# A hybrid decoder layer on one core: four latencies of the planner that orders the attention phase

## The chip, the cores and the metric

The kernel runs on one core of a Trainium2 chip. Times are device microseconds (us) of that core, one launch of the whole layer, and the median of several runs counts. Engines are named as in the profile: PE is TensorE (PEld its weight loads), DVE is VectorE, ACT is ScalarE, POOL is GpSimd, and SP issues most of the DMAs. A bulk product below is one 128x128 by 128x272 matmul of the projections (line L301); a small product is any other matmul.

## The reference, cut to what matters

One decoder layer for a prompt of 512 tokens and for 8 samples of 4 tokens each, in float32, width 1024. Feed-forward, token mixer, feed-forward, each between norms. The change lies in the mixer.

```python
def token_mixer(h, pos, conv_buf, S0, attend, p):
    proj = h @ p['w_in']
    u, z, b_raw, a_raw, q_sw, k_sw, v_sw, gate_a, gate_b = jnp.split(proj, split_idx, axis=-1)
    u, conv_new = short_conv(u, conv_buf, p['conv_w'])        # conv_new is an output, too
    ...
    o_dn, S_new = gated_delta_rule(q_dn, k_dn, v_dn, g, beta, S0)
    o_dn = (rmsnorm(o_dn, p['dn_norm']) * silu(z)).reshape(B, T, DN_V)
    ...
    o_sw, kbuf_new, vbuf_new = attend(q, k, v, p['sinks'])    # prompt: band of 128; sample: cache + own rows
    y = sigmoid(gate_a) * o_dn + sigmoid(gate_b) * o_sw
    return y @ p['w_out'], (kbuf_new, vbuf_new, conv_new, S_new)

def swa_banded(q, k, v, sinks):                               # per group g and 128-query block
    scores = jnp.einsum('bnqkgd,bnskd->bnkgqs', qb, kk) * (SW_HEAD_DIM ** -0.5)
    p = sink_softmax(scores, mask, sinks.reshape(SW_KV_HEADS, SW_GROUP))
    o = jnp.einsum('bnkgqs,bnskd->bnqkgd', p, vv).reshape(B, T, SW_Q)
```

## The kernel before, in words

A float32 product is made of three products of rounded halves: weights arrive by DMA as `raw`, ACT rounds them to `hi` (L270), DVE or POOL takes `lo = raw - hi` (L271), and `mm3` (L301) issues hh*hi, hl*hi and hh*lo, each once for each half of the 544 columns (512 of the prompt, 32 of the samples). So a trace shows pairs of bulk products, and each pair has one weight block.

In the mixer the projections with `w_in` are the main stream. They run in a fixed order of units: four blocks U0 to U3 of the convolved q, k, v of the delta branch, two heads each; between them K, V and the two halves of Q; then eight units G0 to G7 of gates; then `w_out`. Beside the main stream run side streams, all Python generators: two of prompt attention (`attend_stream`, the second one goes on with `attend_sample`), two of the delta rule (`delta_stream`, two heads at a time), one `conv_out` for each head, the delta rule of the samples (`delta_sample`) and the merges.

A planner, class `Streams`, puts all of them in one order. It has a clock `now` in its own units. The main stream yields costs; a side stream yields (cost, latency) between its steps, and its next step falls due when the clock has passed `now + LATK * latency`, with LATK = 1.5. After each step of the main stream every side step that is due is emitted. That order of emission is the priority of the instructions; a scheduler, which has a model of the engines, then fixes the order on each engine. Engines run their queue strictly in that order, and an instruction whose operand isn't there holds up all behind it.

The steps that matter here:

- `conv_block` finishes a head's convolution: ACT copies the projection out (L1183), POOL copies the ends (L1186 to L1189, tile `c`), ACT and DVE make the taps (`y`, L1192, L1194), ACT the tanh (`th`, L1197), DVE the product (`kq` or `vT`, L1198). `conv_out` follows L_CVO later: PE turns `c` (`pco`, L1212), DVE copies it (`so`, L1214), two DMAs write it.
- `attend` does one block of 128 queries for one group of heads: scores `psc` (L1012), mask and maximum on DVE (L1016), the steps L1022 to L1035 on DVE with the exponentials on ACT (L1030), the scaling `s` (L1039 on ACT for one quarter, L1042 on DVE for the rest), the turn of the probabilities on PE (`ppt`, L1051), copies (L1057, L1059), the output `pov` (L1065). There are 16 blocks, eight in each of the two streams, and `ppt` comes 5.5 * L_ATT after the scaling was emitted.
- `attend_sample` does the samples in three items of 3, 3 and 2: scores `pss` (L1098, L1100), softmax, turns `psp`, `psn` (L1126, L1127), then the output products `pso` (L1141, L1146), four groups one straight after the other, then the copies to `osw` (L1150).
- `delta` ends with `pro` (sums of squares), the reciprocal root `ro0y` or `ro1y` on DVE (eleven small instructions, L340 to L345), and 3.5 * L_DN later `prb`, the broadcast of the root by PE (L353), which scales `od` (L1370). Ahead of that, `inverse` inverts 128x128 triangles by substitution on DVE (L1420, L1422), with turned copies `XL` (L1433), and by many small products on PE (`pw` L1440 and L1464, `pz` L1448 and L1478, `pt` L1451 and L1474).

`rope` (L936 to L941) turns the projected queries and keys on DVE. L_ATT is 1.0 and L_DN 0.9.

## Time and profile before

| what | value |
|---|---|
| runs | 1606.12, 1608.23, 1611.68 us; median 1608.23 |
| profiled execution | 1608.77 us, its span 1607.0 us |
| busy, of the span | PE 96%, DVE 55%, ACT 40%, POOL 19% |
| mixer, 720 to 760 us | PE 33.76 of 40 us, DVE 34.61 |
| mixer, 840 to 880 us | PE 38.48 of 40 us, DVE 38.23 |
| granted PE clock, mean of the span | 0.983 |

The profiled execution lies 0.54 us above the median, and 1.77 us of it are outside the span. [...] The views below give, for a stretch, the busy time of each engine and the clock; for an engine, its instructions in order, with the idle time before each and what ended it; and the waits summed up.

### The profile page before, as it was taken

What the parts mean: (1) busy time and instruction counts of PE and PEld (TensorE: products, weight loads), DVE (VectorE), ACT (ScalarE), POOL (GpSimd) and SP (SyncE); (2) the same over time, 40 slices, a digit from 0 to 9 for tenths busy, and PEclk for the clock granted to TensorE, in tenths of its full rate; (3) what the DMA queues carried; (4) which work ended last, traced back from release to release, by engine and by line L of the source; (5) the groups of instructions that cost most, each with busy time, mean ns of one, the idle gap of its engine ahead of it and who ended that gap; (6) DMA issues with size and microseconds to landing.
All of it is one profiled execution on the core that took longest, in us unless ns stands there. A gap on an engine that the chain in (4) does not pass through costs nothing.

```text
span 1607.0 us, 33057 instructions
## 1 busy us (share of the span) xinstructions
PE 1537.5 (96%) x12851; PEld 1418.5 (88%) x12851; DVE 887.6 (55%) x2384; ACT 640.1 (40%) x1449; POOL 305.9 (19%) x443
## 2 busy tenths in 40 slices
PE   7999999999998999998999999999979999999996
PEld 4799999999977999997778888889979999999995
DVE  5433322333598787688889568665474332233365
ACT  4322222222445544445575242223556332223363
POOL 2000000000343231231122134131458000000042
PEclk9999999999999999999999899999999999999998
DMA  9554445445655334653113243624515432333353
GB/s 314 169 183 138 153 136 159 147 148 153 190 167 178 100 75 107 165 135 77 45 45 80 77 121 83 167 55 130 158 53 158 115 86 87 94 87 89 83 152 111
DMA packets 316083, 199.69 MB, mean 124 GB/s; under 512 B 37508, under 2 KB 298335, under 8 KB 315638
## 3 DMA queue, kind: packets, MB, share of 16 engines
q1 hardware_dynamic: 315638, 197.46, 43.5%
q8 instruction: 101, 1.65, 0.4%
q14 instruction: 56, 0.46, 0.1%
q0 software_dynamic: 288, 0.11, 0.0%
HBM read 182.08 MB, written 16.36 MB: 123 GB/s over the span
## 4 chain that ended last, share of the span: by engine, by line
PE 77%; DVE 13%; ACT 3%; DMA 2%; issue 2%; POOL 2%; SPq 0%; DVEq 0%; ACTq 0%; POOLq 0%
PE pg L301 16%; PE pu L301 16%; PE pb L301 16%; PE pd L301 14%; PE adaps L467 3%; DVE y L1194 2%; DVE lo L271 2%; ACT hi L270 1%; PE pov L1065 1%; DVE X L1422 1%; PE pgu L301 1%; DVE s L1016 1%; PE psc L1012 1%; PE pkq L1281 1%; DVE xT L571 1%
## 5 line engine op out<-in xcount | busy, mean ns | idle before, releaser
L270 ACT CAST hi<-raw 128x512 fp32r<-128x512 f32 (+2 forms) x502 | 287.9, 581 | 613.1 <-PE pu L301 172.1
L271 DVE TENSOR_TENSOR lo<-raw,hi 128x512 fp32r<-128x512 f32 (+2 forms) x368 | 252.9, 688 | 385.8 <-ACT hi L270 378.7
L301 PE MATMUL pb<-hh,hi 128*128 128x272 f32 (+1 forms) x1008 | 234.9, 303 | 1.4 <-ACT hi L270 0.7
L271 POOL TENSOR_TENSOR lo<-raw,hi 128x512 fp32r<-128x512 f32 (+1 forms) x104 | 140.6, 1356 | 483.1 <-ACT hi L270 460.5
L301 PE MATMUL pb<-hh,lo 128*128 128x272 f32 (+1 forms) x1008 | 227.7, 296 | 1.3 <-POOL lo L271 0.7
L301 PE MATMUL pb<-hl,hi 128*128 128x272 f32 (+1 forms) x1008 | 227.2, 295 | 1.0 <-DVE hl L271 1.0
L301 PEld LDWEIGHTS pb<-hh,hi 128*128 128x128 f32 (+1 forms) x1008 | 164.6, 191 | 12.0 <-issue 6.5
L301 PE MATMUL pd<-fh,hi 128*128 128x272 f32 x704 | 171.3, 290 | 0.0
L301 PE MATMUL pd<-fl,hi 128*128 128x272 f32 x704 | 170.2, 289 | 0.0
L301 PEld LDWEIGHTS pb<-hl,hi 128*128 128x128 f32 (+1 forms) x1008 | 165.0, 190 | 3.6 <-DVE hl L271 1.5
L301 PEld LDWEIGHTS pb<-hh,lo 128*128 128x128 f32 (+1 forms) x1008 | 164.4, 191 | 4.1 <-DVE lo L271 1.4
L301 PE MATMUL pd<-fh,lo 128*128 128x272 f32 x672 | 162.4, 289 | 4.0 <-POOL lo L271 2.2
L301 PE MATMUL pg<-hh,hi 128*128 128x272 f32 x672 | 149.6, 292 | 7.5 <-ACT hh L538 3.6
L301 PE MATMUL pu<-hh,hi 128*128 128x272 f32 x672 | 148.2, 291 | 0.0
L301 PE MATMUL pg<-hl,hi 128*128 128x272 f32 x672 | 147.0, 289 | 0.3 <-DVE hl L539 0.2
L301 PE MATMUL pu<-hl,hi 128*128 128x272 f32 x672 | 146.1, 289 | 0.0
L301 PE MATMUL pu<-hh,lo 128*128 128x272 f32 x672 | 145.3, 288 | 0.7 <-POOL lo L271 0.7
L301 PE MATMUL pg<-hh,lo 128*128 128x272 f32 x672 | 145.6, 288 | 0.0
L301 PEld LDWEIGHTS pd<-fh,hi 128*128 128x128 f32 x704 | 119.9, 188 | 8.6 <-issue 4.2
L301 PEld LDWEIGHTS pg<-hh,hi 128*128 128x128 f32 x672 | 108.8, 189 | 19.6 <-ACT hh L550 5.0
L301 PEld LDWEIGHTS pd<-fl,hi 128*128 128x128 f32 x704 | 120.2, 188 | 0.0
L301 PEld LDWEIGHTS pd<-fh,lo 128*128 128x128 f32 x672 | 114.1, 188 | 5.6 <-POOL lo L271 2.9
(469 smaller groups left out, 2628.6 us busy)
## 6 DMA issues: line engine op xcount, KB each, us to landing
raw<-w_in SPq DMA_DIRECT2D x136, 256.0 KB, 3.2
wa<-w_ada SPq DMA_DIRECT2D x56, 512.0 KB, 4.4
raw<-ffn_w_gate SPq DMA_DIRECT2D x94, 256.0 KB, 2.9
raw<-ffn_w_up SPq DMA_DIRECT2D x94, 256.0 KB, 7.0
raw<-ffn_w_down SPq DMA_DIRECT2D x92, 256.0 KB, 3.0
wb<-w_ada SPq DMA_DIRECT2D x32, 256.0 KB, 5.8
S<-state_delta SPq DMA_DIRECT2D x8, 512.0 KB, 8.0
delta_sample<-S SPq DMA_DIRECT2D x8, 512.0 KB, 3.4
```

The source lines that it names most:

```text
L270: self.nc.scalar.copy(out=hi, in_=raw)
L271: (eng or self.nc.vector).tensor_tensor(out=lo, in0=raw, in1=hi.bitcast(F32), op=ALU.subtract)
L301: self.nc.tensor.matmul(out=ps[:m, c, :TH], lhsT=a[:r, kt, :m], rhs=b[:r, kx, c * TH:(c + 1) * TH], start=first and i == 0, stop=last and ...
L467: self.ada_mm = nc.tensor.matmul(out=ps[32 * j:32 * j + 32, :], lhsT=self.cT[:, k, :], rhs=was[j], start=k == 0, stop=k == 7, skip_group_c ...
L571: nc.vector.tensor_tensor(out=self.xT[:, b, s], in0=self.xT[:, b, s], in1=t[:, :n], op=ALU.add)
L1012: nc.tensor.matmul(out=ps[:, i * 256:i * 256 + nk], lhsT=self.qT[64 * h:64 * h + 64, 2 * g + i, qb * P:(qb + 1) * P], rhs=self.kd[64 * h:6 ...
L1016: nc.vector.tensor_tensor_reduce(out=s[:, i, :nk], in0=ps[:, i * 256:i * 256 + nk], in1=am[:, lo:], scale=0.125, scalar=-3e38, op0=ALU.add ...
L1065: nc.tensor.matmul(out=po[64 * h:64 * h + 64, :256], lhsT=self.vn[:, c, 64 * g:64 * g + 64], rhs=pTs[kb][:, 2 * h:2 * h + 2, :], start=kb ...
L1194: nc.vector.scalar_tensor_tensor(out=y[:, :CVN], in0=cv[:, i:i + CVN], scalar=w[i], in1=y[:, :CVN], op0=ALU.mult, op1=ALU.add)
L1281: nc.tensor.matmul(out=pv[:, j], lhsT=kq[:, n, 0, c * P:(c + 1) * P], rhs=kq[:, n, :, c * P:(c + 1) * P], start=True, stop=True)
L1422: e.tensor_tensor(out=xs, in0=xs, in1=pv, op=ALU.subtract)
```

## The change

Four constants or yields of the side streams change; no arithmetic does, and the instructions are the same.

- `conv_out` falls due 4.0 instead of 2.0 latencies after it was spawned (3 units of the planner later).
- The first block of each of the two attention streams adds L_FIRST = 6.0 to the latency ahead of its `ppt` (9 units).
- `attend_sample` yields after each of its four groups of output products, with latency L_PSO = 0.6, where it yielded once, after the copies.
- The latency from `pro` to `prb` is 5.0 * L_DN instead of 3.5 * L_DN (2 units).

```diff
-L_CVO = 2.0
+L_CVO = 4.0
+L_FIRST = 6.0
+L_PSO = 0.6
...
-    def attend(self, g, qb, tp):
+    def attend(self, g, qb, tp, first):
...
-        yield 0.0, 5.5 * L_ATT
+        yield 0.0, 5.5 * L_ATT + first * L_FIRST
...
-        for g, qb in items:
-            yield from self.attend(g, qb, tp)
+        for n, (g, qb) in enumerate(items):
+            yield from self.attend(g, qb, tp, n == 0)
...
+                yield 0.2 * n, L_PSO
             for h in range(2):
...
-            yield 0.6 * (n + 1), 0.0
...
-        yield 0.85, 3.5 * L_DN
+        yield 0.85, 5.0 * L_DN
```

Lines of the changed kernel are two higher from the constants on (L301 is L303). Below are pieces of the order that the two programs have on an engine.

First place: PE at the turn of the first two attention blocks, 48 bulk products into G0. Names: `pco` turns a head's conv rows `c`, `ppt` turns the probabilities `s`, `pov` and `psc` are outputs and scores, `pw` belongs to an inverse. Before:

```order
L301 MATMUL pb<-hh,lo 128x272 x2
L1051 MATMUL ppt<-ident,s 128x128 x8
L301 MATMUL pb<-hh,hi 128x272
L1051 MATMUL ppt<-ident,s 128x128 x4
L1065 MATMUL pov<-pT,vn 64x256 x4
L1012 MATMUL psc<-kd,osw 128x256 x4
L1065 MATMUL pov<-pT,vn 64x256 x2
L1012 MATMUL psc<-kd,osw 128x256 x4
L1212 MATMUL pco<-ident,c_8741 81x128
L301 MATMUL pb<-hh,hi 128x272
```

After:

```order
L1214 MATMUL pco<-ident,c_8712 81x128
L303 MATMUL pb<-hl,hi 128x272 x2
L303 MATMUL pb<-hh,lo 128x272 x2
L1053 MATMUL ppt<-ident,s 128x128 x8
L303 MATMUL pb<-hh,hi 128x272
L1053 MATMUL ppt<-ident,s 128x128 x4
L1067 MATMUL pov<-pT,vn 64x256 x4
L1014 MATMUL psc<-kd,osw 128x256 x4
L1067 MATMUL pov<-pT,vn 64x256 x2
L1014 MATMUL psc<-kd,osw 128x256 x4
L1442 MATMUL pw_9144<-XL,O 32x32 x16
L303 MATMUL pb<-hh,hi 128x272
```

The `ppt` have the same bulk product ahead of them as before. Two `pco` of other heads now stand ahead of them, and the one that followed them is gone from there; the first small products of an inverse (`pw`) came up from 50 bulk products further on.

Second place: DVE where the root `ro1y` of the first heads is finished (the three passes are L343 to L345; two lines higher in the changed kernel), beside the rope steps and the delta products `NT`, `AT`. Before:

```order
L936 TENSOR_TENSOR y_8187<-x_8183,cs 128x272
L271 TENSOR_TENSOR lo<-raw,hi 128x512
L937 TENSOR_TENSOR w<-x_8184,cs 128x272
L343 SCALAR_TENSOR_TENSOR ro1a<-rx,ro1y 128x4
L1285 SCALAR_TENSOR_TENSOR NT<-pkq,b_8290,Dm 128x128
L938 TENSOR_TENSOR y_8187<-y_8187,w 128x272
L939 TENSOR_TENSOR x_8184<-x_8184,cs 128x272
L940 TENSOR_TENSOR w<-x_8183,cs 128x272
L344 TENSOR_TENSOR ro1a<-ro1a,ro1y 128x4
L1287 TENSOR_TENSOR AT<-pkq,Dm 128x256
L941 TENSOR_TENSOR x_8184<-x_8184,w 128x272
L345 SCALAR_TENSOR_TENSOR ro1y<-ro1a,ro1y 128x4
```

After:

```order
L347 SCALAR_TENSOR_TENSOR ro1y<-ro1a,ro1y 128x4
L345 SCALAR_TENSOR_TENSOR ro1a<-rx,ro1y 128x4
L346 TENSOR_TENSOR ro1a<-ro1a,ro1y 128x4
L347 SCALAR_TENSOR_TENSOR ro1y<-ro1a,ro1y 128x4
L938 TENSOR_TENSOR y_8187<-x_8183,cs 128x272
L273 TENSOR_TENSOR lo<-raw,hi 128x512
L939 TENSOR_TENSOR w<-x_8184,cs 128x272
L1287 SCALAR_TENSOR_TENSOR NT<-pkq,b_8312,Dm 128x128
L940 TENSOR_TENSOR y_8187<-y_8187,w 128x272
```

The last pass of `ro1y` was behind the rope steps and is now ahead of them. On PE the `prb` that reads it stands 7 bulk products earlier than before.

Third place: PE at the output products of the first sample item (`pso`), in G2. Before:

```order
L301 MATMUL pb<-hh,lo 128x272 x2
L1141 MATMUL pso<-spN,vn 64x48 x2
L1146 MATMUL pso<-spT,vc 64x16 x6
L1141 MATMUL pso<-spN,vn 64x48 x2
L1146 MATMUL pso<-spT,vc 64x16 x6
L1141 MATMUL pso<-spN,vn 64x48 x2
L1146 MATMUL pso<-spT,vc 64x16 x6
L1141 MATMUL pso<-spN,vn 64x48 x2
L1146 MATMUL pso<-spT,vc 64x16 x6
L1474 MATMUL pt_11334<-W,X 32x32 x4
L1478 MATMUL pz_11333<-X,W 32x32 x4
```

After, from the first group to the second:

```order
L1143 MATMUL pso<-spN,vn 64x48 x2
L1148 MATMUL pso<-spT,vc 64x16 x6
L1214 MATMUL pco<-ident,c_10855 81x128
L303 MATMUL pb<-hh,hi 128x272 x2
L303 MATMUL pb<-hl,hi 128x272 x2
L303 MATMUL pb<-hh,lo 128x272 x2
L303 MATMUL pb<-hh,hi 128x272 x2
L303 MATMUL pb<-hl,hi 128x272 x2
L303 MATMUL pb<-hh,lo 128x272 x2
L1480 MATMUL pz_11304<-X,W 32x32 x4
L1488 MATMUL pw_11355<-XL,NT 64x64 x4
L1143 MATMUL pso<-spN,vn 64x48 x2
```

Before, no bulk product stood between the four groups. Now 12 stand between one group and the next, and the same holds for the second and third item. Of the small steps between the groups, `pz` and `pw` belong to an inverse.

Elsewhere the order differs as follows, in bulk products: the first four `pco` stand 24 later; the attention and delta steps that follow the first place stand 10 to 50 earlier; the sample's delta chain stands 36 to 190 later, and its last step, the `prb` of the second half of the heads, 72 later, which leaves 24 bulk products of G7 behind it.

## Rows read from the trace of the kernel before

**Rows 1.** The page: busy time by engine.

```profile
PE 1537.5 (96%) x12851; PEld 1418.5 (88%) x12851; DVE 887.6 (55%) x2384; ACT 640.1 (40%) x1449; POOL 305.9 (19%) x443
```

**Rows 2.** Stretches: length, busy PE, PEld, DVE, ACT, POOL (instructions), PE clock, DMA share, GB/s.

```profile
589.00:617.00 28.00, 23.62 (x176) 22.19 (x176) 26.33 (x80) 11.99 (x21) 7.56 (x21) 1.00 0.33 75
692.00:737.00 45.00, 43.14 (x315) 41.60 (x315) 42.43 (x120) 18.34 (x35) 14.31 (x37) 0.96 0.47 108
744.00:890.00 146.00, 142.01 (x1403) 115.44 (x1402) 128.25 (x540) 90.00 (x285) 25.82 (x58) 0.98 0.24 61
911.00:1076.00 165.00, 159.12 (x1672) 143.33 (x1673) 110.86 (x367) 50.27 (x143) 50.48 (x61) 0.96 0.40 104
```

**Rows 3.** Waits of PE, 560 to 760 us, by releaser: total, times, longest.

```profile
PE ppt L1051 <- issue: 6.1, 1, 6.1
PE pco L1212 <- POOL c L1189: 2.5, 2, 1.8
PE prb L353 <- DVE ro1y L345: 1.9, 1, 1.9
...
PE pb L301 <- ACT cv L1183: 0.5, 1, 0.5
```

**Rows 4.** Timeline of DVE at 617 us: start, length, instruction, idle before, releaser.

```profile
616.88 2.62 DVE L1194 SCALAR_TENSOR_TENSOR y<-cv,cwT,y 128x600 f32<-128x600 f32 x2 [0.94 <-ACT y L1192]
```

**Rows 5.** Timeline of DVE, 697 to 704 us: two passes of the root.

```profile
697.68 0.15 DVE L345 SCALAR_TENSOR_TENSOR ro1y<-ro1a,ro1y 128x4 f32<-128x4 f32 x1
...
702.44 1.22 DVE L345 SCALAR_TENSOR_TENSOR ro1y<-ro1a,ro1y 128x4 f32<-128x4 f32 x1
```

**Rows 6.** Stretches of 4 or 5 us, as in group 2.

```profile
704.00:708.00 4.00, 4.00 (x23) 4.00 (x22) 3.90 (x9) 2.15 (x9) 0.10 (x1) 0.57 0.73 200
745.00:750.00 5.00, 5.00 (x26) 2.83 (x26) 4.78 (x15) 2.65 (x6) 1.26 (x1) 0.64 0.49 131
885.00:890.00 5.00, 5.00 (x84) 4.29 (x83) 3.13 (x6) 1.58 (x3) 0.00 (x0) 0.86 0.22 52
890.00:895.00 5.00, 5.00 (x47) 4.62 (x47) 2.68 (x14) 0.37 (x1) 0.00 (x0) 0.50 0.52 150
895.00:900.00 5.00, 4.98 (x58) 4.37 (x56) 2.21 (x5) 1.85 (x4) 0.21 (x1) 0.96 0.12 33
920.00:925.00 5.00, 5.00 (x44) 4.49 (x42) 0.93 (x8) 1.11 (x3) 0.31 (x1) 0.50 0.18 52
945.00:950.00 5.00, 5.00 (x73) 4.60 (x72) 2.43 (x11) 1.88 (x8) 1.42 (x3) 1.00 0.07 12
```

**Rows 7.** Timeline of DVE, 733 to 744 us: what stands ahead of the scaling.

```profile
733.42 2.60 DVE L1194 SCALAR_TENSOR_TENSOR y<-cv,cwT,y 128x600 f32<-128x600 f32 x3
...
742.32 0.16 DVE L1033 TENSOR_TENSOR den<-den,es 128x4 f32<-128x4 f32 x1 [2.08 <-ACT es L1032]
...
742.93 0.88 DVE L1042 TENSOR_SCALAR s<-s,den 128x256 f32<-128x256 f32 x3
```

**Rows 8.** Timeline of PE, 881 to 890 us: bulk pairs, first and last output products.

```profile
881.20 0.41 PE L301 MATMUL pb<-hl,hi 128*128 128x272 f32 x2
881.46 0.41 PE L301 MATMUL pb<-hh,lo 128*128 128x272 f32 x2
...
886.57 0.32 PE L1141 MATMUL pso<-spN,vn 32*64 32x48 f32 x4
...
889.10 0.83 PE L1146 MATMUL pso<-spT,vc 128*64 128x16 f32 x12
```

**Rows 9.** Timeline of PE, 892 to 894 us: bulk pairs.

```profile
893.51 0.66 PE L301 MATMUL pb<-hh,hi 128*128 128x272 f32 x2
893.96 0.66 PE L301 MATMUL pb<-hl,hi 128*128 128x272 f32 x2
```

**Rows 10.** Timeline of DVE at the samples' merge, 1107 to 1122 us.

```profile
1107.57 0.28 DVE L1675 TENSOR_TENSOR so<-so,prb 128x128 f32<-128x128 f32 x1
...
1121.02 0.34 DVE L1686 SCALAR_TENSOR_TENSOR so<-so,cwT,zs 128x128 f32<-128x128 f32 x1
```

## The prediction

> **What bounds the kernel now.** I read the busy shares first: PE is busy 96% of the span [rows 1], so the kernel can only gain where PE waits or where its clock is at the lower level. The second view is the table of stretches. In 589 to 617 us PE is busy 23.6 of 28 us and DVE 26.3; in 692 to 737 us DVE 42.4 of 45; in 744 to 890 us PE 142.0 and DVE 128.3 of 146 [rows 2]. So in the early part of the mixer, up to the first softmax, DVE is about as full as PE, and a PE wait that the order takes away can come back further on as a wait for DVE. From 911 us DVE has room (110.9 of 165), and time that PE gains there is kept. The third view is the list of PE's waits: one long one of 6.1 us ahead of the first `ppt`, 1.9 us for the root `ro1y` ahead of `prb`, 2.5 us in two for `c` ahead of `pco`, 0.5 us for `cv` [rows 3]. The fourth is the clock in short stretches: it is at 0.50 from late in 885 to 890 until early in 895 to 900 us, and again around 920 to 925, with PE busy 5.00 of 5 us ahead of the first fall [rows 6].
>
> What a fall costs: a pair of bulk products starts 0.25 to 0.26 us after the one before at full clock [rows 8] and 0.45 us at half [rows 9]. The means 0.86, 0.50 and 0.96 [rows 6] make (0.14 + 0.50 + 0.04) x 5 / 0.5 = 6.8 us at half clock, and 6.8 x (1 - 0.25/0.45) = 3.0 us lost.
>
> **The change, part by part.** I call a gain negative.
>
> A. `pco` 24 bulk products (3.0 us) later. The two waits, 1.8 and 0.7 us [rows 3], are for POOL, which makes `c` once ACT has the projection; 3.0 us more is enough for both. But between them PE waits 0.5 us for `cv` [rows 3], and that is tied to DVE, which is busy 26.3 of the 28 us [rows 2]. PE, arriving 1.8 us earlier, waits there 1.8 us longer. Only the second wait is followed by a DVE that itself waits, 0.94 us at 616.88 [rows 4], so that its 0.7 us is kept: -0.7. Bounds 0 (this one is moved too) and -2.5 (both are kept). What `pco` issues comes later too: a copy on DVE and two output DMAs on SP's queue, which nobody reads.
>
> B. `prb` later in the plan. The wait of 1.9 us ends when the last pass of `ro1y` is done. That pass ran at 702.44 for 1.22 us, the pass before at 697.68 for 0.15 us [rows 5]; the rope steps stand between. In the changed order the last pass comes ahead of them, so the root is ready near 698.4 and the wait goes, although `prb` itself stands 7 bulk products earlier. The clock that fell behind the wait (0.57 in 704 to 708 us [rows 6], 4 x 0.43 / 0.5 = 3.4 us at half, 1.5 us lost) probably stays up. That is 3.4 us. But DVE is busy 42.4 of the 45 us up to 737 [rows 2] and does the same work in any order, and the next thing that PE waits for, the first softmax, hangs on DVE. PE gains no more there than DVE's 2.6 idle us, some of which are waits for ACT. I take -1.0; bounds 0 and -3.4.
>
> C. The first `ppt` later. This is what the order doesn't show: both `ppt` keep their place behind the same bulk product, and DVE's queue ahead of the scaling is the same but for a copy of 0.27 us and two steps of the substitution. The wait ends with the chain on DVE: three taps of 2.60 us at 733.42, the maxima, an idle of 2.08 us for the exponentials on ACT, and the scaling at 742.93 [rows 7]. None of it gets shorter, so the wait of 6.1 us stays, and the half clock behind it (0.64 in 745 to 750 us, 3.6 us at half [rows 6], 1.6 us lost). PE comes earlier by what B took away, and waits so much longer. 0; bounds +1.0 (the two `pco` ahead and the copy) and -0.5; were the wait to go, it would give 6.1 + 1.6 = 7.7 us, which is a rival.
>
> D. The output products spread. Before, the four groups run from 886.57 to 889.9 us without a bulk product between [rows 8], and the clock falls inside this block [rows 6]; the second item does the same shortly before 920 us, with a second fall (0.50 in 920 to 925). The third item, a third smaller, ran at 945 to 950 us with the clock at 1.00 [rows 6]. In the changed order 12 bulk products, 1.5 us, stand between one group and the next, in all three items. I expect both falls to go: 2 x 3.0 = -6.0. DVE has room there (2.2 to 3.1 of 5 us [rows 6]), so the gain isn't handed on. Bounds: -6.8, with what the neighbours gain, and 0, if both stay because inverse steps (`pt`, `pz`, `pw`, turns) now lie in the same stretch. The groups' copies into `osw` come some 5 us later; their reader is the samples' merge at 1121.02 [rows 10].
>
> [...]
>
> E. The stretch from 744 to 890 us. Inverse steps of the next heads come up from 50 bulk products further on, and attention and delta steps stand 10 to 50 bulk products earlier. PE's idle time there is 146 - 142.0 = 4.0 us and DVE's 17.7 us [rows 2]. With `pw` now close ahead of the `pz` that need its copy from ACT, I expect one wait of about half a microsecond: an estimate, from the copy's place behind softmax work on ACT. +0.5; bounds -4.0 (all of PE's idle time gone) and +7.7 (a second hole like C's).
>
> F. The sample's delta chain stands 36 to 190 bulk products later. Its waits between 911 and 1076 us are 165 - 159.1 = 5.9 us [rows 2], in many small pieces that move with it. I see nothing in the order that takes them away or adds to them: 0, bounds -4 and +4 (one clock stretch and its neighbours' waits more or less). Its end, the root of the second half, comes 72 bulk products (9.0 us) later. The reader of that root was done at 1107.85 and the merge that needs it ran at 1121.02 [rows 10], so 13.2 us of room cover it; beyond these each microsecond would be paid in full. The state loads and stores of this chain sit on SP's queue ahead of weight loads; they move by the same few microseconds.
>
> Sum: -0.7 - 1.0 + 0 - 6.0 + 0.5 + 0 = -7.2. The profiled execution took 1608.77 us, 0.54 above the median of the runs, so 1601.6 for such an execution, and 1601.0 for the median.
>
> **Rivals.**
>
> 1. The time only moves. DVE takes back A and B, and one or both falls persist because the stretches between the groups are now full of inverse steps, or because the falls don't follow this block at all. For it: DVE's 42.4 of 45 us, and D's untested mechanism. Against: the third item's clock of 1.00, and that PE idles nowhere near the two falls. One fall left: 1601.0 + 3.0 = 1604.0; both: 1607.0, with A and B taken back 1608. That the falls don't follow the block at all has 0.10 of this rival's 0.29.
>
> 2. The change does more than the order says: the first turn finds its probabilities there. That needs DVE to come to the maxima some 6 us earlier, and its queue ahead of them would have to be idle; it idles 2.6 of 45 us. Then 1601.0 - 7.7 = 1593.3.
>
> 3. Slower. The inverse steps that come up put substitution and copies on DVE and ACT ahead of the softmax of the third and later blocks, and PE, which works strictly in order, stands at each `ppt`. The place is 744 to 890 us, where DVE is busy 128.3 of 146 us [rows 2]. There are 14 further blocks. The price is their delay: 0.85 us more on each makes 12 us, which eats the 7.2 and adds 4.8. A single hole like the first costs 7.7 and gives 1608.7; two give 1616.4. Against it: DVE has 17.7 us to spare in that stretch, and the delayed steps are the same in number.
>
> **How the numbers follow.** A median can be told from no change by about 0.3%, 4.8 us: faster is below 1603.4, slower above 1613.1. The forecast has 0.48 (0.42 of it faster, the rest within 0.3%, where A, B or E come out at their poor ends), the first rival 0.29 (0.26 same, 0.03 faster), the second 0.10 (faster), the third 0.13 (0.10 slower, 0.03 same). That makes faster 0.55, same 0.35, slower 0.10. The forecast's own range is 1597 to 1605. Reaching to the first rival's 1608 and most of the second's, and to a single hole, gives 1591 to 1610, with 0.1 left out at each side or less.
>
> **What would show it.** D: granted clock 1.00 through all three items' `pso`, 12 bulk products between the groups. B: no wait at `prb` near 700 us, root done before the rope steps. C: a wait ahead of the first `ppt` of 6 us or more, with a half clock behind. A: no wait at `pco`, and a longer one at `cv`. E: PE idle between 744 and 890 us still near 4 us. I am wrong if the clock falls within the spread groups, if the first wait is gone, or if PE's idle time in that stretch doubles.

## The result, and the profile after

The changed kernel is slower: median 1616.35 us of 20 runs (1604.81 to 1625.47) beside 1608.24 of 20 for the kernel before, ratio 1.0051 with an interval of 1.0038 to 1.0065. The forecast was 1601.0, on the other side, and 1616.35 lies outside its range.

The page of the changed kernel: busy time by engine, which answers [rows 1].

```profile
PE 1541.5 (96%) x12851; PEld 1422.9 (88%) x12851; DVE 895.8 (56%) x2384; ACT 641.0 (40%) x1449; POOL 304.4 (19%) x443
```

The instructions are the same in number. The span is 1611.8 us instead of 1607.0, and PE and DVE are busy 4.0 and 8.2 us longer. The same instructions took longer: PE's go with the lower clock (0.978 instead of 0.983 in the mean of the span), and DVE's are spread over many steps, some of which are looked at below.

Stretches of the changed kernel with the columns of [rows 2] (length, busy PE, PEld, DVE, ACT, POOL, PE clock, DMA share, GB/s). The first four answer [rows 2], the next two [rows 6] at the first turn, the next two at the first two sample items. The last three are the updates of the sample states.

```profile
589.00:617.00 28.00, 24.82 (x183) 23.06 (x182) 26.61 (x79) 12.26 (x21) 7.61 (x21) 1.00 0.33 79
692.00:737.00 45.00, 40.92 (x310) 39.37 (x309) 43.44 (x128) 18.69 (x37) 16.63 (x37) 0.99 0.46 107
744.00:890.00 146.00, 138.49 (x1346) 114.01 (x1345) 129.58 (x539) 90.08 (x284) 25.73 (x58) 0.98 0.25 64
911.00:1076.00 165.00, 161.95 (x1596) 146.54 (x1595) 111.70 (x367) 53.71 (x149) 38.51 (x56) 0.94 0.40 105
...
740.00:745.00 5.00, 1.33 (x7) 1.36 (x8) 2.51 (x17) 5.00 (x22) 0.21 (x1) 0.50 0.29 66
745.00:750.00 5.00, 5.00 (x23) 3.11 (x22) 4.71 (x18) 2.71 (x6) 1.27 (x1) 0.52 0.75 194
...
890.00:895.00 5.00, 5.00 (x81) 4.39 (x79) 4.30 (x10) 1.98 (x4) 0.31 (x1) 1.00 0.25 64
...
920.00:925.00 5.00, 5.00 (x44) 5.00 (x43) 4.87 (x12) 2.11 (x6) 0.46 (x1) 1.00 0.06 21
...
1010.00:1015.00 5.00, 2.70 (x15) 2.00 (x15) 4.97 (x5) 0.19 (x1) 3.78 (x3) 1.00 0.20 55
1015.00:1020.00 5.00, 5.00 (x71) 3.81 (x70) 4.20 (x13) 1.33 (x4) 0.00 (x0) 0.66 0.74 205
...
1025.00:1030.00 5.00, 5.00 (x23) 2.39 (x23) 1.80 (x4) 0.00 (x0) 0.00 (x0) 0.50 0.27 80
```

The two falls of the clock at the output products are gone. In exchange the clock is low for longer around the first turn, and it falls at 1016 us, where the kernel before had 1.00 up to 1031 us.

Waits of PE in the changed kernel between 560 and 760 us (total, times, longest), which answer [rows 3].

```profile
PE pco L1214 <- DVE mx L1018: 4.1, 1, 4.1
PE ppt L1053 <- issue: 4.0, 1, 4.0
...
PE pb L303 <- ACT cv L1185: 1.4, 2, 0.8
```

The 1.9 us for the root and the 2.5 us for `c` are gone, and the wait ahead of the first `ppt` is 4.0 instead of 6.1 us. New is one of 4.1 us ahead of a `pco`, ended by DVE's maxima `mx`. Three timelines of the changed kernel show how it comes about: POOL, PE and DVE.

```profile
729.89 0.22 POOL L1191 COPY c<-cv 128x24 f32<-128x24 f32 x1
```

```profile
727.76 1.57 PE L1014 MATMUL psc<-kd,osw 64*128 64x256 f32 x12
...
736.88 0.50 PE L1214 MATMUL pco<-ident,c 128*81 128x128 f32 x1 [4.08 <-DVE mx L1018]
...
743.67 1.73 PE L1053 MATMUL ppt<-ident,s 128*128 128x128 f32 x7 [4.03 <-issue]
```

```profile
736.05 0.42 DVE L1018 CUSTOM_DVE_ANT_0 s<-psc,cst 128x256 f32<-128x256 f32 x1
736.39 0.08 DVE L1018 DVE_READ_ACCUMULATOR2_ANT mx<- 128x1 f32 x1
736.39 0.42 DVE L1018 CUSTOM_DVE_ANT_0 s<-psc,cst 128x256 f32<-128x256 f32 x1
736.74 0.08 DVE L1018 DVE_READ_ACCUMULATOR2_ANT mx<- 128x1 f32 x1
...
742.38 0.16 DVE L1035 TENSOR_TENSOR den<-den,es 128x4 f32<-128x4 f32 x1 [3.35 <-ACT es L1034]
...
743.00 0.88 DVE L1044 TENSOR_SCALAR s<-s,den 128x256 f32<-128x256 f32 x3
```

`c` was there at 730.11, more than six microseconds before the `pco`. What was missing is a place to write to: in the code `pco` takes a buffer of the same four-buffer PSUM ring `wk` as the scores `psc`, and the scores of the first two blocks (727.76) sit in all four until DVE has read them (the first of the four by 736.82). The scaling of the probabilities comes at 743.00, as before (742.93, [rows 7]), so the first `ppt` gains nothing.

The other new wait stands among the updates `psu` of the sample states. Ahead of these updates POOL multiplies the states by their decays, four instructions for half of the heads: POOL's scaling, below. Timelines of the changed kernel: PE, DVE and POOL.

```profile
1013.85 1.95 PE L1663 MATMUL psu<-vm,skdec 32*128 32x512 f32 x4 [2.30 <-DVE vm L1656]
...
1025.01 3.78 PE L1663 MATMUL psu<-vm,skdec 32*128 32x512 f32 x4
...
1033.29 1.98 PE L1663 MATMUL psu<-vm,skdec 32*128 32x512 f32 x4
```

```profile
1006.06 0.35 DVE L1641 TENSOR_SCALAR svn<-pvn,sb 128x128 f32<-128x128 f32 x1 [1.29 <-PE pvn L1639]
1006.33 2.17 DVE L273 TENSOR_TENSOR lo<-raw,hi 128x512 fp32r<-128x512 f32 x1
1008.42 2.43 DVE L1528 SCALAR_TENSOR_TENSOR z<-tg,z 128x544 f32<-128x544 f32 x1
1010.77 2.93 DVE L1656 TENSOR_TENSOR vm<-svn,cst 128x1024 f32<-128x1024 f32 x1
...
1015.23 0.68 DVE L273 TENSOR_TENSOR lo<-raw,hi 128x512 fp32r<-128x512 f32 x1
```

```profile
1004.16 8.47 POOL L1660 TENSOR_TENSOR S<-S,sgrow 128x1024 f32<-128x1024 f32 x4 [1.69 <-PE pks L1632]
```

While POOL scales the sample states (8.47 us), DVE takes 2.17 us for a `lo` that takes 0.68 five microseconds later, and `vm`, for which PE waits, ends some 5 us late: 1.5 us more for `lo`, 1.7 each for `z` and `vm`, which take 0.72 and 1.22 us in the changed kernel without that scaling (below). In the kernel before, `vm` stood beside the scaling, too, and took less, 2.31 us (its timelines of DVE and POOL):

```profile
987.18 2.31 DVE L1654 TENSOR_TENSOR vm<-svn,cst 128x1024 f32<-128x1024 f32 x1
```

```profile
984.17 9.01 POOL L1658 TENSOR_TENSOR S<-S,sgrow 128x1024 f32<-128x1024 f32 x4
```

Behind `vm`, in the changed kernel, the updates follow one another with 12 bulk products between them where the order of before has 24, and a `psu` at the lower clock takes 3.78 instead of 1.98 us.

The clock, from stretches of three profiled executions of each of the two kernels (both were run again for it):

| stretch, us | before | after | half clock before, us | after, us |
|---|---|---|---|---|
| 735 to 755, first turn | 0.83, 0.83, 0.83 | 0.66, 0.66, 0.66 | 6.8 | 13.6 |
| 885 to 930, output products | 0.85, 0.96, 0.89 | 1.00, 1.00, 1.00 | 9 | 0 |
| 1010 to 1050, state updates of after | 0.91, 1.00, 0.87 | 0.74, 0.66, 0.74 | 6 | 23 |
| 1165 to 1205, end of the mixer | 0.96, 0.87, 0.87 | 0.79, 0.87, 0.79 | 8 | 15 |

Time at half clock is (1 - clock) x length / 0.5, the mean of three. Full and half are the two levels seen: of 3214 stretches of 0.5 us in the first profile of the kernel before the clock is 1.00 in 3091, 0.50 in 104 and in between in 19, where it changes (after: 3078, 127 and 18 of 3223). In the kernel before the updates of the third row stand at 987 to 1007 us, at 1.00 in all three profiles, and its falls in that row come behind them, from 1030 us. Over the 20 runs each the time at half clock is 74 us in all after and 56 before, by each run's clock and span. Through all runs of this study, with a level of its own for each kernel, a microsecond at half clock costs 0.35 us (a run is 1.5 us off that line). So 18 or 19 us more at half clock are some 6.5 of the 8 us lost.

Counting bulk products from the start of the span in the two profiled traces gives the rest of the picture. With 4592 started (the next one comes at 729.6 us before) the changed kernel is 3.5 us ahead, with 4640 (745.2) level, with 4940 (864.9) 0.1 behind. With 5240 (949.0) it is 7.4 ahead, part of it sample work that stands later now. With 6032, at the end of G7 (1118.3), all that has been done and it is 0.1 ahead. From there on the order on PE is the same, and by 1264 us it is 4.8 behind, all of it from 1165 to 1205 us.

One pair of profiles carries this only so far: the other two of the kernel before stand 8.0 and 0.2 us ahead of the first at the end of G7. In the means of three the changed kernel is 4.0 us behind there and 6.9 at 1264 us. So some 4 us are lost by the end of G7, where it should have been ahead by what the output products give, and some 3 us from 1165 to 1205 us.

### The profile page after: what moved, and what is told of

It is laid out like the page before. It is cut to its first block, busy times and chain, and to the rows that moved or that the text cites. A ratio compares the mean times of both kernels' runs of the same rounds, so it can differ in the third digit from the quotient of the medians.

```text
span 1611.8 us, 33047 instructions
## 1 busy us (share of the span) xinstructions
PE 1541.5 (96%) x12851; PEld 1422.9 (88%) x12851; DVE 895.8 (56%) x2384; ACT 641.0 (40%) x1449; POOL 304.4 (19%) x443
## 4 chain that ended last, share of the span: by engine, by line
PE 77%; DVE 14%; DMA 3%; ACT 2%; issue 2%; POOL 1%; SPq 0%; DVEq 0%; POOLq 0%; ACTq 0%
PE pb L303 16%; PE pg L303 15%; PE pu L303 15%; PE pd L303 14%; PE adaps L469 3%; DVE y L1196 2%; DVE lo L273 2%; PE psu L1663 1%; PE pgu L303 1%; PE pov L1067 1%; DVE X L1424 1%; ACT hi L272 1%; PE psc L1014 1%; PE ppt L1053 1%; DVE pr L1422 1%
## 5 line engine op out<-in xcount | busy, mean ns | idle before, releaser
L303 PE MATMUL pb<-hh,hi 128*128 128x272 f32 (+1 forms) x1008 | 234.9, 303 | 2.7 <-ACT cv L1185 1.4
L273 POOL TENSOR_TENSOR lo<-raw,hi 128x512 fp32r<-128x512 f32 (+1 forms) x104 | 137.2, 1323 | 486.5 <-ACT hi L272 463.0
L303 PE MATMUL pb<-hl,hi 128*128 128x272 f32 (+1 forms) x1008 | 227.1, 295 | 1.0 <-DVE hl L273 1.0
L303 PE MATMUL pb<-hh,lo 128*128 128x272 f32 (+1 forms) x1008 | 226.4, 295 | 1.5 <-POOL lo L273 0.7
L303 PEld LDWEIGHTS pb<-hh,hi 128*128 128x128 f32 (+1 forms) x1008 | 163.8, 190 | 11.6 <-issue 4.8
L303 PE MATMUL pd<-fh,hi 128*128 128x272 f32 x704 | 172.0, 291 | 0.0
L303 PE MATMUL pd<-fl,hi 128*128 128x272 f32 x704 | 170.8, 290 | 0.0
L303 PEld LDWEIGHTS pb<-hh,lo 128*128 128x128 f32 (+1 forms) x1008 | 164.1, 190 | 4.4 <-DVE lo L273 1.7
L303 PEld LDWEIGHTS pb<-hl,hi 128*128 128x128 f32 (+1 forms) x1008 | 164.5, 190 | 3.0 <-DVE hl L273 1.5
L303 PE MATMUL pd<-fh,lo 128*128 128x272 f32 x672 | 162.9, 290 | 2.6 <-DVE lo L273 2.4
L303 PE MATMUL pg<-hh,hi 128*128 128x272 f32 x672 | 150.5, 294 | 7.9 <-ACT hh L540 3.6
L303 PE MATMUL pu<-hh,hi 128*128 128x272 f32 x672 | 149.1, 292 | 0.3 <-DVE fhx L611 0.3
L303 PE MATMUL pg<-hl,hi 128*128 128x272 f32 x672 | 147.8, 291 | 0.2 <-DVE hl L541 0.2
L303 PE MATMUL pu<-hl,hi 128*128 128x272 f32 x672 | 146.8, 290 | 0.0
L303 PE MATMUL pu<-hh,lo 128*128 128x272 f32 x672 | 145.8, 289 | 0.7 <-POOL lo L273 0.7
L303 PE MATMUL pg<-hh,lo 128*128 128x272 f32 x672 | 146.1, 289 | 0.0
L303 PEld LDWEIGHTS pd<-fh,hi 128*128 128x128 f32 x704 | 120.4, 189 | 8.6 <-issue 4.2
L303 PEld LDWEIGHTS pg<-hh,hi 128*128 128x128 f32 x672 | 109.4, 190 | 19.8 <-issue 6.3
L303 PEld LDWEIGHTS pd<-fl,hi 128*128 128x128 f32 x704 | 120.8, 189 | 0.0
L303 PEld LDWEIGHTS pd<-fh,lo 128*128 128x128 f32 x672 | 114.6, 189 | 4.2 <-DVE lo L273 3.3
```

Of the source, the lines that this page charges most:

```text
L273: (eng or self.nc.vector).tensor_tensor(out=lo, in0=raw, in1=hi.bitcast(F32), op=ALU.subtract)
L303: self.nc.tensor.matmul(out=ps[:m, c, :TH], lhsT=a[:r, kt, :m], rhs=b[:r, kx, c * TH:(c + 1) * TH], start=first and i == 0, stop=last and ...
```

## Each part alone, and the change without one part

Two theories at first: the sample's chain, moved into another stretch, loses what D gains (theory S in the expectations); or the new `pco` wait and its longer half clock do (P). A third is that the clock simply falls differently from order to order (C).

The six edits, each of one part: `only_` kernels are the kernel before with it, `all_but_` kernels the changed one without it.

```diff
 # cvo                    # first                   # dn
-L_CVO = 2.0              -L_FIRST = 0.0            -3.5 * L_DN
+L_CVO = 4.0              +L_FIRST = 6.0            +5.0 * L_DN
 # pso
+                yield 0.2 * n, L_PSO
-            yield 0.6 * (n + 1), 0.0
```

Only the output products spread:

> The kernel before with one part of the change alone: the sample's output products yield after each group (L_PSO). Up to the first of them the order on PE is that of before; behind it the sample's delta chain stands 12 to 170 bulk products later, and its eight state updates of a half (psu<-vm) stand 12 bulk products apart where 24 stood before. Theory S (the packed state updates let the clock fall in 1010 to 1045 us, and that costs more than the two falls in the pso blocks gave): no clock fall in the pso blocks, half clock for 12 us or more at the state updates, time 1.003 to 1.006 of before. Theory P (the loss comes from pco, which waits for a PSUM buffer that psc holds, ahead of the first softmax turn): pco stands as before, so the two falls that go are a plain gain, 0.995 to 0.998. What the prediction held: 0.996.

All but that:

> The changed kernel with the output products in one piece again; the first softmax, pco and prb stay as in the changed kernel, the sample's delta chain is back at its old place. Theory S: the loss goes, 0.999 to 1.001 of before, with the falls in the pso blocks back and at most 7 us of half clock between 1010 and 1045 us. Theory P: the loss stays, 1.004 to 1.007, with the 4 us wait of pco for the maxima.

Only `conv_out` later:

> The kernel before with L_CVO = 4.0 alone: pco later. Two pco come to stand ahead of the first ppt, one of them ahead of it by 9 bulk products, as in the changed kernel. Theory P: PE waits about 4 us at pco for DVE's maxima (mx) and then about 2 to 4 us at ppt, the half clock begins 5 us earlier, time 1.002 to 1.005. Theory S: the ppt comes at the same time as before (the two waits together end with the scaling), so only the longer half clock behind it counts, 1 to 1.5 us: 0.999 to 1.001.

All but that:

> The changed kernel with L_CVO back at 2.0: the pco ahead of the first ppt is gone but for one; sample chain, output products and prb as in the changed kernel. Theory S: the loss stays, 1.003 to 1.006. Theory P: the loss goes, 0.996 to 1.000.

Only `prb` later, and only the first `ppt` later:

> The kernel before with the latency from pro to prb at 5.0 * L_DN alone. The root's last pass comes ahead of the rope steps, no pco ahead of the first turn, updates of the first half 24 apart. The prediction's B: no wait at prb, PE 3 to 4 us earlier at 730 us, all but 1 us of it gone again by 750 us, because the first turn hangs on DVE: 0.998 to 1.001. Theory C (each reordered kernel has more half clock): 1.002 or more.

> The kernel before with L_FIRST = 6.0 alone. The first turn keeps its place, as in the prediction's C; one pco of another head comes ahead of it by 10 bulk products, the inverse steps come up to the first turn, the sample chain comes 36 bulk products earlier, its updates of the first half 24 apart and of the second 12. Expected by C and E: a wait at pco for the maxima and a longer half clock at the turn, +1 to +2 us; 1.000 to 1.003. Theory C as it stands: 1.002 or more.

| kernel | median, us | ratio (interval) |
|---|---|---|
| only the output products | 1617.29 | 1.0050 (1.0032 to 1.0068) |
| all but these | 1613.48 | 1.0036 (1.0021 to 1.0051) |
| only `conv_out` | 1615.89 | 1.0051 (1.0033 to 1.0068) |
| all but this | 1615.72 | 1.0044 (1.0026 to 1.0061) |
| only `prb` | 1609.31 | 1.0016 (1.0001 to 1.0030) |
| only the first `ppt` | 1611.51 | 1.0030 (1.0017 to 1.0044) |
| the changed kernel again | 1617.33 | 1.0052 (1.0031 to 1.0072) |

Every part alone is slower. Alone they lose 1.5% together, in one kernel 0.5%: the losses don't add, so they are not four prices of four edits. Neither theory is enough: only the output products and all but `conv_out` came out as S said, and the two others lose 0.36% and 0.51% where S had at most 0.1%. P comes close for these two and misses the first two. Waits of PE, 560 to 760 us, in the kernel with only `conv_out` later, then with only `prb` later:

```profile
PE ppt L1053 <- issue: 4.0, 1, 4.0
PE pco L1214 <- DVE mx L1018: 3.4, 1, 3.4
```

```profile
PE ppt L1053 <- issue: 8.9, 1, 8.9
PE pco L1214 <- POOL c L1191: 2.5, 2, 1.8
```

The `pco` wait belongs to A: 3.4 us with `conv_out` alone. But it is 2.0 with the later `ppt` alone and 4.2 with all but `conv_out`, since either order puts a `pco` behind the scores. With only `prb` later the root's 1.9 us are gone and the first `ppt` waits 8.9 instead of 6.1 us, which is what B and C said of each other.

With only the output products spread, PE's timeline at the state updates is this:

```profile
1017.23 3.50 PE L1663 MATMUL psu<-vm,skdec 32*128 32x512 f32 x4 [4.36 <-DVE S L1666]
1025.09 3.78 PE L1663 MATMUL psu<-vm,skdec 32*128 32x512 f32 x4
1033.48 3.78 PE L1663 MATMUL psu<-vm,skdec 32*128 32x512 f32 x4
```

Here D alone is enough for a wait of 4.4 us and three slow updates in a row (3.50, 3.78 and 3.78 us). The sample's chain is where D's gain goes. What DVE stands for ahead of these `S` steps is a DMA: it idles 2.81 us, up to 1014.90, until `sgrow`, the decays of the second half of the heads, has landed. POOL's scaling reads the tile of that name for the first half, and the DMA is issued at 1011.53 us, when the scaling has ended (1011.50). In the kernel before it is the same (issued at 993.21, the scaling ended at 993.18), but DVE idles 1.80 us and no wait of PE follows.

The changed kernel was timed again beside these:

> The changed kernel again, unaltered, for a second profile and for the granted clock of each timed run. Theory S as it stood is too small, since the kernels without the packed state updates were slow too. Theory C: the time of a run goes with the time that it spends at half clock, about 0.33 to 0.45 us for each us, and each of the reordered kernels spends more there than the one before (mean clock 0.978 or less against 0.983); the falls at the sample's state updates (1010 to 1045 us) and at the first softmax turn come in each profile, those between 1170 and 1200 us only in some. Theory W: the loss is idle time of PE; then two profiles agree in their waits, and the mean clock differs from before's by no more than 0.002.

It is slower by as much again, 1.0052. In all three of its profiles the clock is low around the first turn and at the updates, and the mean is 0.977 or 0.978. That is theory C for the changed kernel; for the others it doesn't hold throughout (below).

## The updates apart

The changed kernel with half as much latency again ahead of each update of the first half:

```diff
-            yield 0.0, 1.0 * L_SMP
+            yield 0.0, (1.5 if hg == 0 else 1.0) * L_SMP
```

> The changed kernel with one latency of the sample's delta chain raised (1.0 to 1.5 ahead of each state update of the first half), so that the updates psu<-vm stand 24 to 36 bulk products apart instead of 12; all ahead of them on PE is as in the changed kernel; the chain's second half ends 72 bulk products later, behind the last gate unit. Theory S (narrowed to: the packed updates are the largest part of the loss): the wait of 2.3 us for vm or S and the 20 us of half clock from 1016 us go to 7 us or less, 1.000 to 1.003 of before, at least 0.002 below the changed kernel. Rival L: what the chain loses by its late end (its root now comes when the merge needs it) takes that back, 1.004 to 1.007.

Median 1610.88, ratio to the kernel before 1.0032 (1.0014 to 1.0050): 3 us back by the ratios, 5.5 by the medians, with intervals that overlap. The stretch from 1010 to 1110 us, in this kernel, then in the changed one:

```profile
1010.00:1110.00 100.00, 97.82 (x969) 83.42 (x970) 71.83 (x172) 28.54 (x72) 26.09 (x27) 1.00 0.44 124
```

```profile
1010.00:1110.00 100.00, 97.59 (x894) 81.46 (x894) 64.02 (x162) 23.14 (x63) 24.99 (x26) 0.90 0.40 110
```

PE is as busy in both, and at a clock of 1.00 it gets 75 more matmuls done. At the end of G7 this kernel is 9.9 us ahead of the first profile of the kernel before. Then the samples' merge, now late, holds PE for 4.1 us at 1119 us; only 3.4 us are left by 1265 us. So the updates' place is a part of the loss, and the room at the chain's end isn't free.

With `conv_out` back as well, and the output products yielding only in the first two items (the next section's edit):

> The changed kernel with L_CVO back at 2.0, the third item in one piece and the state updates of the first half 24 to 36 apart; one pco is still ahead of the first turn. Both known losses cut down: 0.998 to 1.001, with no fall from 1010 to 1045 us, half clock of 10 to 14 us at the first turn and a wait of up to 2 us for the sample's merge near 1119 us. If spacing only moves the loss to the end of the chain: 1.003.

1616.16, 1.0051 (1.0036 to 1.0065). Here the `pco` wait is 4.1 us still (the later `ppt` is in), and the clock falls for 13.7 us at 1088 us instead; its profiled run has a mean clock of 0.977, the changed kernel's 0.978. Spacing by a constant moves the hole as much as it mends it.

## The output products spread less

The kernel before with other yields: after every second group (`before_halves`); or after each group of the first two items, the third whole as before (`two_items`); and the latter with `prb` later.

```diff
 # before_halves
+                if g % 2:
+                    yield 0.4 * n, L_PSO
 # two_items
+                if n == 3:
+                    yield 0.2 * n, L_PSO
+            if n == 2:
+                yield 0.6 * (n + 1), 0.0
```

> The kernel before, with the sample's output products yielding after two groups instead of after each (no other part): the delta chain of the samples moves by 48 bulk products instead of 130 to 190, and its state updates stay 24 apart. Theory S: no packed updates, so no wait of more than 1 us there and 3 to 10 us of half clock in all between 1010 and 1085 us; the pso falls partly gone; 0.997 to 1.001 of before. Rival: any shift of the chain costs (only_pso's 1.005): 1.003 or more.

> The kernel before with one part of the change, and that cut down: the output products yield after each group in the first two items alone; the third stays in one piece and yields as before. The order on PE is that of before up to the first of them; the sample's state updates stand 24 bulk products apart (the last pair 12), the chain's end 48 later. If the gain of D was real and only the packed updates took it back: no fall in the first two pso blocks, no wait over 1 us and at most 10 us of half clock at the updates, 0.996 to 0.999 of before. If any shift of the sample chain costs (as the kernel with two halves had it, 1.0046, with a wait of 6.7 us for svn): 1.002 to 1.005, with a wait of PE for DVE of over 3 us somewhere in the chain.

> As the kernel with two spread items, with the latency from pro to prb at 5.0 * L_DN besides. Gain of D real and kept: 0.996 to 0.999, with a longer wait at the first turn (8 to 9 us, as with that latency alone) that eats what prb gives. Any shift costs: 1.002 to 1.005.

Medians 1614.08 (1.0046, 1.0031 to 1.0061), 1610.64 (1.0026, 1.0016 to 1.0036) and 1612.88 (1.0038, 1.0023 to 1.0052). All slower, although `two_items` has the updates of the first half as far apart as before, but for the last pair. Its timelines of DVE and POOL show what they share:

```profile
994.51 1.88 DVE L1427 TENSOR_TENSOR X<-X,pr 32x64 f32<-32x64 f32 x1
996.32 0.67 DVE L273 TENSOR_TENSOR lo<-raw,hi 128x512 fp32r<-128x512 f32 x1
...
997.53 1.92 DVE L1425 TENSOR_TENSOR pr<-X,B 32x63 f32<-32x63 f32 x1
999.48 1.83 DVE L1427 TENSOR_TENSOR X<-X,pr 32x63 f32<-32x63 f32 x1
1001.35 1.83 DVE L1425 TENSOR_TENSOR pr<-X,B 32x60 f32<-32x60 f32 x1
1003.21 0.21 DVE L1427 TENSOR_TENSOR X<-X,pr 32x60 f32<-32x60 f32 x1
1003.35 0.27 DVE L1639 TENSOR_TENSOR sR<-svs,pks 128x128 f32<-128x128 f32 x1
```

```profile
994.40 8.71 POOL L1663 TENSOR_TENSOR S<-S,sgrow 128x1024 f32<-128x1024 f32 x4 [0.75 <-PE pks L1635]
```

Four steps of a substitution take 1.83 to 1.92 us instead of 0.21, and all four lie inside POOL's scaling. `sR` stands behind them on DVE, and PE waits 7.65 us for it. That made a new theory (G): DVE is held up by POOL's scaling, and what it costs depends on which DVE steps the order happens to put there. These kernels agree:

| kernel | POOL's scaling, us | slow DVE steps in it | PE's longest wait behind |
|---|---|---|---|
| before | 984.2 + 9.0 | `lo` 1.28 and 1.07, `vm` 2.31, `stq` 2.00 | under 1 us |
| after | 1004.2 + 8.5 | `lo` 2.17, `z` 2.43, `vm` 2.93 | 2.3 us, `psu` |
| only the first `ppt` | 979.7 + 7.8 | `osw` 2.00, `pr` 1.47, `X` 1.84, `pr` 1.85 | 4.6 us, `poT` |
| every second group | 985.8 + 8.4 | `osw` 2.20, `pr`, `X`, `pr` 1.83 to 1.87 | 6.7 us, `poT` |
| only `prb` | 973.7 + 7.5 | four of the substitution, 1.83 to 1.92 | 4.8 us, `pvn` |
| `two_items` | 994.4 + 8.7 | four of the substitution, 1.83 to 1.92 | 7.7 us, `pvn` |

Three of them have no more half clock than the kernel before: 48 us in the mean of the runs with only the first `ppt` later, 51 in `two_items` and 55 with every second group, beside 56. So their loss is not the clock's, and the waits of 4.6 to 7.7 us are large enough for it.

Two kernels don't fit the theory. With only `conv_out` later (992.2 + 9.0) and with all but the output products (988.7 + 9.0) the scaling covers `lo`, `vm` and `stq` as before and no long wait follows, and yet they lose 0.51% and 0.36%. The first one's profile shows 2.5 us lost at the first turn, with the `pco` wait; for the second the cause stays open.

Each of POOL's instructions takes 1.9 to 3.1 us (1.91 to 2.90 before, 1.92 to 2.90 after, 1.90 to 3.09 in `two_items`), and a small DVE step takes 1.83 to 1.92 there. Not each step is held up: in the changed kernel `svn`, with one tensor input and that in PSUM, took 0.35 at 1006.06 and `sR` 0.29 at 1004.48, and in `two_items` `lo` took 0.67 at 996.32. Around that `lo` two slow steps end 3.06 us apart (996.39 and 999.45), where the next two end 1.86 and 1.87 us later; the longest of POOL's instructions in that kernel, 3.09 us where the median is 1.92, fits that place. What the two engines contend for, and which of them goes first, isn't shown by these runs.

## POOL's scaling taken away

The test of it: POOL doesn't scale the sample states any more; DVE multiplies and adds in one instruction for each sample. In three kernels: `two_items`, the changed one, and the one before.

```diff
-            nc.gpsimd.tensor_tensor(out=S0[h], in0=S0[h], in1=E4[:, h, :, ST - 1:ST].to_broadcast([P, SB, P]), op=ALU.mult)
...
-                sv = S0[h][:, s0:s0 + 4, :]
-                nc.vector.tensor_tensor(out=sv, in0=sv, in1=p3.rearrange("p (s v) -> p s v", s=4), op=ALU.add)
+                for s in range(s0, s0 + 4):
+                    nc.vector.scalar_tensor_tensor(out=S0[h][:, s, :], in0=S0[h][:, s, :], scalar=E4[:, h, s, ST - 1:ST],
+                                                   in1=p3[:, (s - s0) * P:(s - s0 + 1) * P], op0=ALU.mult, op1=ALU.add)
```

> The kernel with two spread items (two_items), and the scaling of the sample states taken off POOL: its eight products of 128x1024 go, and DVE scales within the update instead (eight 128x128 instructions of S*E + psu for each head where two of 128x512 added psu). The order on PE is that of two_items but for a few bulk products. Theory G (PE's waits in the sample chain come from DVE being slowed while POOL scales the states, 1.8 to 2.9 us where 0.2 to 0.7 are normal): the wait of 7.6 us for sR goes to 1 us or less, DVE's steps of the inverse there take 0.2 us again, 0.995 to 0.999 of before. Rival: DVE's queue is simply too full there (its own order); the wait stays above 4 us, and DVE's 9 us more make it 1.003 or worse.

> The changed kernel with the scaling of the sample states taken off POOL in the same way; its order on PE stays. Theory G: the wait of 2.3 us for vm goes; the packed updates and their half clock from 1016 us stay (they come from the packing), so 1.002 to 1.004. If POOL was the cause of the falls too: 1.000 or less.

> The kernel before with the scaling of the sample states taken off POOL in the same way, its order on PE unchanged. It had no wait of over 1.4 us there, so theory G gives little: 0.997 to 1.001. Where the fused updates cost DVE more than POOL's slowing did: 1.001 to 1.003.

| kernel | median, us | ratio to before (interval) | with POOL's scaling (ratio) |
|---|---|---|---|
| `two_items`, fused | 1603.51 | 0.9966 (0.9951 to 0.9982) | 1610.64 (1.0026) |
| changed kernel, fused | 1607.89 | 0.9997 (0.9976 to 1.0019) | 1616.35 (1.0051) |
| kernel before, fused | 1609.12 | 1.0002 (0.9979 to 1.0025) | 1608.24 |

The edit is worth nothing in the kernel before and 7.1 and 8.5 us in the two others. The same steps on DVE in `two_items` without the scaling:

```profile
1000.24 0.20 DVE L1425 TENSOR_TENSOR pr<-X,B 32x63 f32<-32x63 f32 x1
1000.48 0.21 DVE L1427 TENSOR_TENSOR X<-X,pr 32x63 f32<-32x63 f32 x1
1000.73 0.21 DVE L1425 TENSOR_TENSOR pr<-X,B 32x60 f32<-32x60 f32 x1
...
1001.11 0.27 DVE L1639 TENSOR_TENSOR sR<-svs,pks 128x128 f32<-128x128 f32 x1
```

And PE's wait for `sR` in it, 911 to 1130 us:

```profile
PE pvn L1642 <- DVE sR L1639: 1.0, 1, 1.0
```

DVE does more here (eight `S` steps of 2.15 us in all for a head instead of two of 1.28 us in all), and PE's wait still falls from 7.65 to 1.0 us.

In the changed kernel `vm` takes 1.22 us instead of 2.93 and the `psu` wait is gone. Its order on PE is the same but for a few places. With the same work done at the end of G7 it is 7 us ahead of the mean of the changed kernel's three profiles. It has 59 us at half clock in the mean of its runs where the changed kernel has 74, and at 0.35 us each these 15 us are 5 of the 8.5. From 1010 to 1050 us the clock is 0.87 instead of 0.66 to 0.74. One fall among the updates stays: 0.50 from 1020 to 1030 us, with PE busy 39.69 of 40 us from 1010 to 1050 and a `psu` of 3.78 us, so this one doesn't come from POOL's scaling. The 4.1 us ahead of `pco` and the 0.66 at the first turn are as before the edit.

So POOL's scaling is shown to be what makes the difference between slower and level for the changed kernel. Two things stay unproven. The edit takes away the slowed steps and the DMA of `sgrow` that waits for POOL, and doesn't tell them apart; for `two_items` and the changed kernel the rows put the slowed steps ahead of the wait. And the gain of D doesn't show on top in the changed kernel, though the interval leaves room for 4 us. In the kernel before, fused, that DMA now waits, by the code, for DVE's own updates: DVE idles 3.92 us for it and PE 2.9 us for `sNT` behind it, 1.4 before, which may be why the edit gives nothing there. The first of the three, at 1603.51, beats both kernels.

## Why the prediction was wrong

**D, right about the falls, too large in price.** Both falls at the output products went, in all three profiles, and the third item stayed at 1.00. With the old yields put back into the changed kernel the falls are there again (894.5 and 925.2 us). So the case that they don't follow this block (0.10 of the first rival) is out. But -6.0 was read from one profile, with 13.6 us at half clock. The mean of three is 9, since one fall didn't come in the second profile and two others were half as long, and by the prediction's own price that is 4.0 us. In `two_items` without POOL's scaling only inverse steps stand between the first two groups of the first item, and a short fall stays there (0.96 from 885 to 930 us).

PE was busy 5.00 of 5 us ahead of the first fall [rows 6], and what went with the falls was small work in one piece. The fall at the first turn stands otherwise: it comes at 741.7 us, within PE's wait of 6.1 us that ends at 743.60. So a wait is not what all of them have in common, and what sets the clock isn't shown by these runs.

**F, the step that failed.** The chain that was moved 36 to 190 bulk products I set at 0 with 4 us each way, because the order took away no wait and added none that I could see. It lost all of D's gain and more: 8.5 us lie between the changed kernel and the same without POOL's scaling, twice F's upper bound of 4. Two things were missed. The updates moved closer, 12 instead of 24 bulk products, which the order shows and I didn't weigh. And a duration of the trace of before doesn't travel with its instruction: `vm` at 2.31 us stood in that trace beside POOL's 9.0 us of scaling, and nothing asked what would stand there next. The 13.2 us of room at the chain's end did hold in the changed kernel; with 1.5 times the latency it no longer did.

**A, wrong in its mechanism.** The waits for `c` went, and `cv` waits rose from 0.5 to 1.4 us, as forecast. Not seen: a later `pco` falls behind the scores, whose four buffers it needs. 4.1 us, where I had 0 to -2.5. The wait itself costs little, since the first `ppt` stands for the scaling of the probabilities anyway (743.67 us, 743.60 before), but the clock falls at 736 us instead of 742. I checked whether `c` was there, not whether its output had a place. That this place is a PSUM buffer is read from the code and the releaser; a kernel with a buffer of its own for `pco` wasn't tried.

**B and C, right.** No wait at `prb`, root done at 698.57 before the rope steps; and what was won went into the wait ahead of the first `ppt` (8.9 us with B alone). My -1.0 for B was too much. C's half clock of 3.6 us was read from 745 to 750 us alone, and with the stretch ahead of it is 6.8. With A's 4.1 us, PE stands 8.1 us there instead of 6.1, and the clock is low for 13.6 us instead of 6.8. At 865 us the changed kernel is 0.1 behind: A, B, C and E together came to 0 instead of -1.2, and A and B were taken back, as the first rival said.

**E, small as forecast.** PE's idle time from 744 to 890 us is 146 - 138.5 = 7.5 us instead of 4.0, nearly the doubling that I had named as a sign against me. But the bulk products are as level at 865 us as they were at 745, and so the third rival, which put a loss into this stretch, isn't what made the kernel slower. That its price for two holes, 1616.4, is nearly the time measured is chance: the waits and falls stand elsewhere.

**What stays open.** The falls from 1165 to 1205 us differ from run to run of one kernel, and are longer after (15 against 8 us) with the same order on PE. I can't say what sets them. They are most of the 4.8 us between the first two profiled executions, and some 3 of the 7 us between the means of three. Nor is it shown why all but the output products, with neither D nor a new wait in the sample's chain, still loses 0.36%.

## What to carry over

Ahead of moving a chain, look at what runs on POOL and DVE together at the new place, and price the moved steps by rows that stand beside the same neighbour. For each matmul that moves, ask for two things: its operand and its output buffer. Where every reordering loses a little, look for work on another engine that the present order only happens to avoid, and take that away first: with POOL's scaling gone, the order that had lost 0.26% won 0.34%. And where the clock falls differently from run to run, price a fall from more than one profile.

## What the chip showed that was not expected

- A DVE step of 0.21 us (32x63) takes 1.83 to 1.92 beside POOL's scaling, a `lo` of 0.68 takes 2.17: 1.5 to 1.7 us more in these, small or large. Others there took 0.4 to 1.1 more (`lo` 1.07 and 1.28, `vm` 2.31 in the kernel before) or nothing.
- The clock fell with PE busy: in the changed kernel without POOL's scaling PE was busy 39.69 of the 40 us from 1010 to 1050, and the clock was 0.87, which is 10.4 us at half, among updates 12 bulk products apart. It needn't: in the changed kernel updates of the second half, some of them 12 apart too, ran at 1.00 (1093 to 1109 us, a `psu` of 1.98 us), and with half as much latency again in the first half the clock was 1.00 from 1010 to 1110 us.
- One kernel's runs spread by 1.3% (1604.81 to 1625.47 after), and the time at half clock explains most of it: 0.35 us for each microsecond, with 1.5 us left over.
